# Block-pair loads of a matmul with rotary embedding: all in fp32 quarters over SyncE and ScalarE, in twelve groups instead of ten

## The chip, the core and the metric

The kernel runs on one core of one Trainium2 chip. The metric is the device time of one execution in microseconds (us), lower is better. The engines are named as in the profile: PE is TensorE (PEld its weight loads), DVE VectorE, ACT ScalarE, POOL GpSimd, SP SyncE. SP, ACT and POOL can issue DMA transfers; each has its own queue, and all queues are served by the same 16 DMA engines.

## What is computed

```python
x: (16, 512, 768) fp32, weight: (768, 768) fp32, cos, sin: (512, 64) fp32, n_heads = 12
y = np.matmul(x, weight).reshape(16, 512, 12, 64)
y1, y2 = y[..., :32], y[..., 32:]
out1 = y1 * cos1 - y2 * sin1      # cos1, sin1: first half of the head, cos2, sin2: second
out2 = y2 * cos2 + y1 * sin2
out = np.concatenate([out1, out2], axis=-1).reshape(16, 512, 768)
```

## The kernel before

The 8192 rows of x are cut into 64 tiles of 128 rows, in 16 groups of four (`QB`). The contraction of 768 is cut into six chunks of 128 (`CHUNKS`). The kernel computes in fp16 with fp32 sums, so each tile of x has to be loaded, cast to fp16 and turned (rows to columns) before PE can use it as the stationary operand. A group's result fills six PSUM banks (`py`).

There are two ways for the rows of x to get in.

- A plain tile: `load` (line 201) brings 128 x 768 fp32 by one DMA of SP, 384 KB in pieces of 3072 bytes; `cast` (236) makes fp16 on ACT; `turn_rows` (256) turns it on PE by twelve half-height transposes (line 266) and ACT copies the result out of PSUM (line 185 by way of `copy`).
- A block pair: the third and fourth tile of a group, which are two tiles of a batch pair, together. `load_quarter` (209) brings them in four DMAs, one for each 32 partitions, in pieces of 192 elements, so that a 32 x 32 block transpose on DVE (`turn_pair`, 282, line 294) is all the turning needed; PE and the PSUM copies are left out.

`BLOCKS` (137) says which pairs go that way: the second pair of groups 5 to 14, ten in all. In odd groups the quarters come over SP as fp32 in 768-byte pieces into one of three buffers `xb`, and ACT casts the pair in one instruction to `xd` (`cast_pair`, 274), which DVE then turns. In even groups POOL issues the quarters, the DMA casts on the way, fp16 pieces of 384 bytes land in one of three buffers `xh`, and DVE turns from there.

A matmul step takes one tile. In groups 1 to 14 each matmul uses 64 rows of the contraction, and two lines of them run through PE a little apart (`walk`, `one`, `both`; line 359). `rope` multiplies PSUM by cos and sin on DVE (line 411) and adds the halves on POOL (line 428) into `ov`, one of four group buffers. `store` (line 449) writes half a group, 768 KB, by one DMA, mostly issued by ACT.

Everything is ordered by hand. `Flow.do` gives an instruction to its engine in program order and adds the semaphore waits that its reads and writes need; so an instruction that waits holds back all that is behind it on its engine, and DMAs are issued by the engine's own instruction stream. The main loop runs over the tiles i = 4 to 63. In each step it gives PE the matmuls, then `bturns` (block pairs turned by DVE, four tiles ahead), `turns` (plain tiles, three to four ahead), `casts` (five ahead), `pool_loads` (the POOL quarters, 20 ahead), and the stores that the table `stores` (603) puts at this step. For groups 3 to 10 those are the steps 4(g+2) and 4(g+2)+2. SP's loads are a list of their own (`fetch`, 471): tiles in order, with one quarter put behind a tile from the group before a pair on; `pump` (487) issues from it whenever a cast has freed a buffer, with at most ten tiles and three pairs in hand.

In ACT's stream the order within four steps is: copy of the first plain tile turned, cast of the pair (in groups that have one over SP), copy of the second, a store, the casts of two plain tiles, a store.

The lines of the loop that set this order:

```python
        bturns(i + B_AHEAD)
        turns(i + 1 + (T_AHEAD if i > QB else 2), 1)
        casts(i + 1 + (C_AHEAD if i > QB else 4), 1 + i % 2)
        pool_loads(i + P_AHEAD)
        for q in stores.get(i, ()):
            store(*q)
```

Of the kernel before, what the change touches and what calls it, by code (L numbers as in the profile page):

```python
# [10 lines left out]
FP32 = mybir.dt.float32  # L11
FP16 = mybir.dt.float16
# [4 lines left out]
class Flow:  # L17
# [24 lines left out]
    def do(self, e, make, reads=(), writes=(), dma=None, tick=True, after=0):  # L42
        need = {}
        for k in reads:
            for s, v in self.wrote.get(k, {}).items():
                need[s] = max(need.get(s, 0), v)
        for k in writes:
            for d in (self.wrote, self.readby):
                for s, v in d.get(k, {}).items():
                    need[s] = max(need.get(s, 0), v)  # L50
        if e == "pe":
            need.pop("pe", None)
            if after:
                need["pe"] = after
        waits = self.settle(e, need)
        for s, v in waits[:-1]:
            self.eng[e].wait_ge(self.sem(s), v)  # L57
        i = make(self.eng[e])
        if waits:
            s, v = waits[-1]  # L60
            i.wait_op(self.sem(s), v, "sem-ge")
        name, step = (dma, 16) if dma else (e, 1)
        self.sem(name)
        at = self.count[name] + step
        if tick or dma:
            i.then_inc(self.sems[name], step)
            self.count[name] = at
            self.known[name, at] = dict(self.seen[e])
        for k in reads:
            d = self.readby.setdefault(k, {})  # L70
            d[name] = max(d.get(name, 0), at)
        for k in writes:
            self.wrote[k] = {name: at}
            self.readby[k] = {}
        return i
# [30 lines left out]
def kernel(  # L106
# [11 lines left out]
    f = Flow(nc, tc)  # L118
    do = f.do
    P = nc.NUM_PARTITIONS  # L120

    B, S, H = x.shape
# [4 lines left out]
    NQ = P // R  # L127
    NT = H // (2 * P)
    SB = S // P
    QB = 4  # L130
# [4 lines left out]


    BLOCKS = {}
    for g in range(5, 15):
        BLOCKS[g, 1] = "pool" if g % 2 == 0 and g >= 4 else "sp"

    def sbuf(name, shape, dt):
        return nc.alloc_sbuf_tensor(name, shape, dt).ap()

    NX, NB, NBH, NC, NCP, NXT, NXP, NOV = 10, 3, 3, 5, 2, 8, 4, 4

    ident = sbuf("ident", [P, P], FP16)
    cold = sbuf("cold", [P, 512], FP16)
# [3 lines left out]
    w_sb = sbuf("w_sb", [P, NT, 2, H], FP16)  # L151
    xs_b = [sbuf(f"xs{i}", [P, H], FP32) for i in range(NX)]
    xb_b = [sbuf(f"xb{i}", [P, 2 * H], FP32) for i in range(NB)]
    xh_b = [sbuf(f"xh{i}", [P, 2 * H], FP16) for i in range(NBH)]
    xc_b = [sbuf(f"xc{i}", [P, H], FP16) for i in range(NC)]
    xd_b = [sbuf(f"xd{i}", [P, 2 * H], FP16) for i in range(NCP)]
    xt_b = [sbuf(f"xt{i}", [P, NT, 2, P], FP16) for i in range(NXT)]
# [20 lines left out]
    def ring(name, n, state={}):  # L178
        k = state.get((id(f), name), 0)
        state[id(f), name] = k + 1  # L180
        return k % n
# [6 lines left out]
    def where(i):  # L188
        g, s = divmod(i, QB)
        return QB * (g // SB) + s, g % SB  # L190

    def pair_of(i):
        return i // QB, (i % QB) // 2

    def is_block(i):
        return pair_of(i) in BLOCKS

    xs, xc, xT = {}, {}, {}
# [10 lines left out]
    def load_quarter(gh, q):  # L209
        g, h = gh  # L210
        b, r = where(g * QB + 2 * h)
        e = BLOCKS[gh]
        src = x[b : b + 2].rearrange("b (j a r) (q k) -> r q a (b j) k", r=SB, a=R, q=NQ)
        if q == 0:
            xs[gh] = ring("xh", NBH) if e == "pool" else ring("xb", NB)
        k = xs[gh]
        name = f"xh{k}" if e == "pool" else f"xb{k}"
        buf = xh_b[k] if e == "pool" else xb_b[k]
        dst = buf.rearrange("p (j k) -> p j k", j=2 * NQ)
        do(e, lambda eng: eng.dma_start(out=dst[ts(q, R)], in_=src[r, q]),  # L220
           writes=[f"{name}q{q}"], dma=name)

    wv = weight.rearrange("(p t e) n -> t e p n", t=NT, e=2)

# [49 lines left out]
    def cast_pair(gh, e="act"):  # L274
        k = xs[gh]
        c = ring("xd", NCP)
        xc[gh] = c
        do(e, copy(e, xd_b[c].rearrange("p (t j e) -> p t j e", t=NT, e=2),
                   xb_b[k].rearrange("p (j t e) -> p t j e", t=NT, e=2)),
           reads=[f"xb{k}q{q}" for q in range(NQ)], writes=[f"xd{c}"])  # L280

    def turn_pair(gh):
        g, h = gh
        z = ring("xp", NXP)
        dst = xp_b[z].bitcast(FP32)
        if BLOCKS[gh] == "pool":
            k = xs[gh]
            src = xh_b[k].bitcast(FP32).rearrange("p (j t) -> p t j", t=NT)
            rd = [f"xh{k}q{q}" for q in range(NQ)]
        else:  # L290
            c = xc[gh]
            src, rd = xd_b[c].bitcast(FP32), [f"xd{c}"]
        v = xp_b[z].rearrange("p (t m e) -> p t e m", t=NT, e=2)
        do("dve", lambda eng: eng.transpose(out=dst, in_=src), reads=rd, writes=[f"xp{z}"])  # L294
        for s in (0, 1):
            xT[g * QB + 2 * h + s] = (
                lambda t, e, s=s: v[:, t, e, ts(s, P)], f"xp{z}")
# [171 lines left out]


    fetch, quarters = [], []
    soon = [p for p in sorted(BLOCKS) if BLOCKS[p] == "sp"]
    for i in range(QB, NTILE):
        if soon and i >= max(2, soon[0][0] - 1) * QB:
            quarters += [(soon[0], q) for q in (0, 2, 1, 3)]
            soon.pop(0)
        if not is_block(i):
            fetch.append(i)
            if quarters:
                fetch.append(quarters.pop(0))  # L480
        elif quarters and quarters[0][0] == pair_of(i):
            fetch.append(quarters.pop(0))
# [40 lines left out]
    def castx(i, e):  # L523
        cast(i, e)
        xs_used[0] += 1
# [33 lines left out]
    pump()  # L559

    rows_on = [False]
    state = {"cast": 4, "turn": 4, "bturn": 0, "pool": 0}
    pairs = sorted(BLOCKS)
    pool_pairs = [p for p in pairs if BLOCKS[p] == "pool"]

    def casts(upto, most=NTILE):
        while state["cast"] < min(upto, NTILE) and most > 0:
            most -= 1
            i = state["cast"]
            state["cast"] += 1  # L570
            if not is_block(i):
                castx(i, "act")
            elif i % 2 == 0 and BLOCKS[pair_of(i)] == "sp":
                cast_pair(pair_of(i))
                xb_used[0] += 1
            pump()
# [9 lines left out]
    def bturns(upto):  # L586
        while state["bturn"] < len(pairs):
            gh = pairs[state["bturn"]]
            if gh[0] * QB + 2 * gh[1] >= upto:
                return  # L590
            turn_pair(gh)
            state["bturn"] += 1

    def pool_loads(upto):
        while state["pool"] < len(pool_pairs):
            gh = pool_pairs[state["pool"]]
            if gh[0] * QB + 2 * gh[1] >= upto:
                return
            for q in (0, 2, 1, 3):
                load_quarter(gh, q)  # L600
            state["pool"] += 1

    stores = {}
    for g in range(LAST):
        for h in (0, 2):
            i = QB * (g + 1) + h
            q = (g, h * H, (h + 2) * H, "act")
# [4 lines left out]
            elif g < LAST - 2:  # L612
                i = QB * (LAST - 2) + 2 * (g - LAST + 4) + h // 2
            else:
                q = q[:3] + ("sp",)
            stores.setdefault(i, []).append(q)

    C_AHEAD, T_AHEAD, B_AHEAD, P_AHEAD = 5, 3, 4, 20

    for i in (0, 1):  # L620
        mm0(i, CHUNKS[5])
# [15 lines left out]
    for i in range(QB, NTILE):  # L637
        g, s = divmod(i, QB)
        us = units(g)
        done_to = (s + 1) * H  # L640
        rows_on[0] = QB <= i < QB * LAST - 1
        if g < LAST:
            if s % 2 == 0:
                for r in range(2):
                    lines[r].extend(walk(i // 2, r))
            for n in range(1, 4):
                both((i - QB) * 4608 + n * 1536)
                if n == 1 and i > QB:
                    turns(i + T_AHEAD, 1)
        if i == QB * LAST:  # L650
            both(NTILE * 4608)
        for p in pieces(g, s) if g == LAST else ():
            a, z, _, bank = p
            for c in CHUNKS:
                mm_piece(i, p, c, c == CHUNKS[0], c == CHUNKS[-1],
                         tick=c == CHUNKS[-1])
            for u in us:
                if u[1] == z:
                    rope(g, u)
        bturns(i + B_AHEAD)  # L660
        turns(i + 1 + (T_AHEAD if i > QB else 2), 1)
        casts(i + 1 + (C_AHEAD if i > QB else 4), 1 + i % 2)
        pool_loads(i + P_AHEAD)
        for q in stores.get(i, ()):
            store(*q)
        if g == LAST:
            if s == 2:
                store(g, 0, H, "sp")
            if s == 3:
                store(g, H, 2 * H, "act")  # L670
# [4 lines left out]
    for k, add in enumerate(late):  # L675
        c = 3 * H + 256 + 256 * k
# [38 lines left out]
```

## Time and profile before

| What | Value |
|---|---|
| Time, median of 3 runs | 152.34 us (152.06 to 155.32) |
| The profiled execution's own time | 151.85 us |
| Its span (first to last instruction) | 150.1 us |
| Granted TensorE clock, mean | 0.986 of full speed |
| Busy: PE, DVE, POOL, ACT | 140.7, 126.9, 123.0, 77.9 us |
| Bytes moved by DMA | 51.27 MB, 342 GB/s over the span |
| Queue of SP, of ACT, of POOL | 27.92, 21.10, 1.97 MB |
| Issue to landing, median: tile, fp32 quarter, fp16 quarter, store by ACT | 17.3, 17.4, 12.8, 8.8 us |
| Idle of ACT before its copies, waiting for PE's turns | 43.5 us |
| Idle of POOL before its adds, waiting for DVE | 18.8 us |

How to read it: a busy PE in the table does not say that PE is the bound; the chain of work that ended last does, since it follows each step back to what released it. The DMA view cut to a window counts, for each queue, the packets sent (the pieces of the transfers, and small closing ones), the bytes, and the share of the time of 16 DMA engines; the shares of several queues overlap and can sum to more than 100%. The bytes of POOL's queue are those written (fp16); it reads twice as many. In the timeline an engine's rows show start, length, line, what is written from what, and in brackets the idle time ahead with what ended it; rows with a q behind the engine (ACTq, SPq) are DMA issues.

### The profile page before, as it was taken

How to read it: one execution, taken by the hardware profiler on the slowest of the kernel's cores; microseconds unless marked ns; L12 is line 12 of the kernel's file. 1: busy time of each engine (PE TensorE's matmuls, PEld its weight loads, DVE VectorE, ACT ScalarE, POOL GpSimd, SP SyncE). 2: the span in 40 equal slices, each digit the busy share in tenths (PEclk: the TensorE clock that was granted, in tenths of full speed). 3: DMA queues.
4: the chain of work that ended last, by engine and by line, in shares of the span. 5: the costliest groups of instructions: out<-in, count | busy, mean ns of one | idle time of the engine just before them, and what ended most of it. 6: DMA issues, size and time to landing. Idle time of an engine off the chain costs nothing.

```text
span 150.1 us, 4381 instructions
## 1 busy us (share of the span) xinstructions
PE 140.7 (94%) x1938; PEld 101.4 (68%) x1938; DVE 126.9 (85%) x92; ACT 77.9 (52%) x92; POOL 123.0 (82%) x68
## 2 busy tenths in 40 slices
PE   6879999999999999999999999999999999999930
PEld 2445567777787777777777777777777777776620
DVE  0245989887888899999999998999989998999990
ACT  3453888787777924456262905293327626264000
POOL 1000495999989988999999999999996979999990
PEclk9999999999999999999999999999999999999995
DMA  4999999999999999999999999999999999966574
GB/s 125 393 391 398 404 401 390 274 404 275 319 367 327 347 354 361 285 397 332 359 346 392 355 332 359 370 391 319 356 367 412 415 406 399 385 269 235 217 296 144
DMA packets 27556, 51.27 MB, mean 342 GB/s; under 512 B 7185, under 2 KB 13073, under 8 KB 27537
## 3 DMA queue, kind: packets, MB, share of 16 engines
q1 hardware_dynamic: 14592, 27.92, 53.8%
q10 hardware_dynamic: 7504, 21.10, 35.5%
q0 software_dynamic: 5440, 1.97, 10.6%
q8 instruction: 15, 0.25, 0.6%
q14 instruction: 5, 0.03, 0.1%
HBM read 27.79 MB, written 25.17 MB: 353 GB/s over the span
## 4 chain that ended last, share of the span: by engine, by line
PE 87%; DMA 4%; DVE 4%; SPq 1%; issue 1%; ACT 1%; DVEq 0%
PE py L359 73%; PE py L334 8%; PE pt L266 4%; DMA w_raw<-in_weight_dram 4%; DVE tq L411 2%; PE pt L251 1%; DVE ov L428 1%; SPq L205 1%; SPq L227 1%; ACT xt L185 1%; DVE xs L411 0%; DVE w_sb L185 0%; SPq L710 0%; DVEq L57 0%; SPq L116 0%
## 5 line engine op out<-in xcount | busy, mean ns | idle before, releaser
L428 POOL TENSOR_TENSOR ov<-tq 128x1536 f32<-128x1536 f32 (+3 forms) x30 | 76.3, 2564 | 18.9 <-DVE tq L411 18.8
L359 PE MATMUL py<-w_sb,xt 64*128 64x256 f16 (+1 forms) x864 | 80.7, 323 | 0.0
L411 DVE TENSOR_TENSOR tq<-py,csn 128x1024 f32<-128x1024 f32 (+2 forms) x46 | 74.8, 1656 | 5.4 <-PE py L359 5.0
L359 PEld LDWEIGHTS py<-w_sb,xt 64*128 64x128 f16 x864 | 53.2, 94 | 17.8 <-DVE tq L411 0.4
L185 ACT COPY xt<-pt 128x768 f16<-128x768 f16 x42 | 33.6, 801 | 47.8 <-PE pt L266 43.5
L359 PE MATMUL py<-w_sb,xp 64*128 64x256 f16 (+1 forms) x480 | 46.8, 323 | 0.0
L185 ACT CAST xc<-xs 128x768 f16<-128x768 f32 x44 | 39.1, 909 | 12.1 <-DMA xs<-in_x_dram 12.0
L411 DVE TENSOR_TENSOR w_raw<-py,csn 128x1024 f32<-128x1024 f32 (+1 forms) x21 | 35.2, 1676 | 4.4 <-PE py L359 4.2
L428 POOL TENSOR_TENSOR ov<-w_raw 128x1536 f32<-128x1536 f32 (+1 forms) x12 | 35.0, 2926 | 3.6 <-DVE w_raw L411 3.4
L359 PEld LDWEIGHTS py<-w_sb,xp 64*128 64x128 f16 x480 | 30.4, 94 | 9.5
L334 PE MATMUL py<-w_sb,xt 128*128 128x256 f16 (+1 forms) x90 | 15.7, 323 | 1.3 <-DVE w_sb L185 1.1
L266 PEld LDWEIGHTS pt<-ident,xc 64*128 64x128 f16 x432 | 14.1, 95 | 1.9 <-ACT xt L185 0.6
L334 PEld LDWEIGHTS py<-w_sb,xt 128*128 128x128 f16 x90 | 8.1, 98 | 7.2 <-DVE w_sb L185 2.7
L266 PE MATMUL pt<-ident,xc 64*128 64x64 f16 x432 | 12.3, 190 | 0.3 <-ACT xt L185 0.3
L220 POOL DMA_DIRECT2D xh<-in_x_dram x20 | 11.7, 590 | 0.0
L185 ACT CAST xd<-xb 128x1536 f16<-128x1536 f32 x5 | 8.2, 1637 | 0.0
L294 DVE STREAM_TRANSPOSE xp<-xh 128x768 f32<-128x768 f32 x5 | 6.2, 1241 | 0.0
L510 PE MATMUL py<-cold 128*128 128x512 f16 x12 | 4.8, 569 | 1.4 <-DVE cold L453 1.4
L185 DVE CAST w_sb<-w_raw 128x768 f16<-128x768 f32 x6 | 3.3, 558 | 3.3 <-DMA w_raw<-in_weight_dram 3.3
L185 DVE COPY xt<-pt 128x768 f16<-128x768 f16 x2 | 1.1, 558 | 5.2 <-PE pt L251 5.2
L294 DVE STREAM_TRANSPOSE xp<-xd 128x768 f32<-128x768 f32 x5 | 4.8, 969 | 0.0
L251 PEld LDWEIGHTS pt<-ident,xc 128*128 128x128 f16 x48 | 3.2, 104 | 2.1 <-ACT xc L185 1.3
(16 smaller groups left out, 14.5 us busy)
## 6 DMA issues: line engine op xcount, KB each, us to landing
out_dram<-ov ACTq DMA_DIRECT2D x26, 768.0 KB, 8.8
xs<-in_x_dram SPq DMA_DIRECT2D x44, 384.0 KB, 17.3
xb<-in_x_dram SPq DMA_DIRECT2D x20, 192.0 KB, 17.4
out_dram<-ov SPq DMA_DIRECT2D x4, 768.0 KB, 3.7
w_raw<-in_weight_dram SPq DMA_DIRECT2D x6, 384.0 KB, 6.9
xh<-in_x_dram POOLq DMA_DIRECT2D x20, 96.0 KB, 12.8
out_dram<-ov SPq DMA_DIRECT2D x1, 384.0 KB, 2.3
out_dram<-ov ACTq DMA_DIRECT2D x1, 384.0 KB, 2.3
```

The lines of the kernel that those rows point to most:

```text
L185: eng.copy(out=o, in_=i_) if e == "act" else eng.tensor_copy(out=o, in_=i_)
L205: do(e, lambda eng: eng.dma_start(out=xs_b[k], in_=x[b].rearrange("(p r) h -> r p h", r=SB)[r]), writes=[f"xs{k}"], dma=f"xs{k}")
L220: do(e, lambda eng: eng.dma_start(out=dst[ts(q, R)], in_=src[r, q]), writes=[f"{name}q{q}"], dma=name)
L227: do(e, lambda eng: eng.dma_start(out=w_raw[:, t, h], in_=wv[t, h]), writes=[f"wr{t}{h}"], dma=f"w{t}{h}")
L251: do("pe", lambda eng: eng.transpose(pt[:, t, h, :], src[:, t, h, :], ident), reads=[f"xc{c}", "ident"], writes=[f"pt{k}"], tick=(t, h) == ...
L266: do("pe", lambda eng: eng.transpose(pts[r][:, t, h, :], src[rows, t, h, :], ident[rows, rows]), reads=[f"xc{c}", "ident"], writes=[f"pt{r ...
L294: do("dve", lambda eng: eng.transpose(out=dst, in_=src), reads=rd, writes=[f"xp{z}"])
L334: do("pe", lambda eng: eng.matmul(ps, get(t, h), w_sb[:, t, h, a - s * H : z - s * H], start=start, stop=stop), reads=[key, f"w{t}{h}"], w ...
L359: do("pe", lambda eng: eng.matmul(py[:, a:z], get(t, h)[rows], w_sb[rows, t, h, a - s * H : z - s * H], start=start, stop=not opens and en ...
L411: do("dve", lambda eng: eng.tensor_tensor(out=tq.rearrange("p j (h d) -> p j h d", d=D), in0=ps.rearrange("p (h d) -> p h d", d=D) .unsque ...
L428: do(adder, lambda eng: eng.tensor_tensor(out=ov_b[o][:, ds(c0, w)].rearrange("p (h t d) -> p h t d", t=2, d=HD), in0=tq[:, 0].rearrange(" ...
L510: do("pe", lambda eng: eng.matmul(py[:, ts(b, 512)], cold[:, 0:P], cold, start=True, stop=warmed[0] < WARM - 6), reads=["cold"], writes=[f ...
```

## The change

- `BLOCKS` now holds the second pair of groups 3 to 14, twelve pairs, all fp32; POOL issues no loads, and the fp16 buffers `xh` are gone. There are four `xb` buffers for three.
- Of each pair, quarters 0 and 1 are issued by SP out of the `fetch` list, and quarters 2 and 3 by ACT, in the main loop after the casts of a step and ahead of its stores. Quarter 2 is issued 11 tile steps and quarter 3 nine tile steps before the pair's first tile (later for the first pairs: from steps 4 and 5 on). The cast of a pair waits for all four quarters, as before.
- All pairs are cast by ACT into `xd` and turned by DVE from there.

```diff
-    for g in range(5, 15):
-        BLOCKS[g, 1] = "pool" if g % 2 == 0 and g >= 4 else "sp"
+    for g in range(3, 15):
+        BLOCKS[g, 1] = "sp"
...
-    NX, NB, NBH, NC, NCP, NXT, NXP, NOV = 10, 3, 3, 5, 2, 8, 4, 4
+    NX, NB, NC, NCP, NXT, NXP, NOV = 10, 4, 5, 2, 8, 4, 4
...
     def load_quarter(gh, q):
         g, h = gh
         b, r = where(g * QB + 2 * h)
-        e = BLOCKS[gh]
         src = x[b : b + 2].rearrange("b (j a r) (q k) -> r q a (b j) k", r=SB, a=R, q=NQ)
-        if q == 0:
-            xs[gh] = ring("xh", NBH) if e == "pool" else ring("xb", NB)
-        k = xs[gh]
-        name = f"xh{k}" if e == "pool" else f"xb{k}"
-        buf = xh_b[k] if e == "pool" else xb_b[k]
-        dst = buf.rearrange("p (j k) -> p j k", j=2 * NQ)
+        k = xs[gh] = sorted(BLOCKS).index(gh) % NB
+        dst = xb_b[k].rearrange("p (j k) -> p j k", j=2 * NQ)
+        e = "sp" if q < 2 else "act"
         do(e, lambda eng: eng.dma_start(out=dst[ts(q, R)], in_=src[r, q]),
-           writes=[f"{name}q{q}"], dma=name)
+           writes=[f"xb{k}q{q}"], dma=f"xb{k}{e}")
...
-            quarters += [(soon[0], q) for q in (0, 2, 1, 3)]
+            quarters += [(soon[0], q) for q in (0, 1)]
...
-            elif i % 2 == 0 and BLOCKS[pair_of(i)] == "sp":
+            elif i % 2 == 0:
                 cast_pair(pair_of(i))
...
+    pieces_at = {}
+    for n, (g, h) in enumerate(pairs):
+        for q, lead in ((2, 11), (3, 9)):
+            pieces_at.setdefault(max(QB + 2 * n + q - 2, g * QB + 2 * h - lead), []).append(((g, h), q))
...
-        pool_loads(i + P_AHEAD)
+        for piece in pieces_at.get(i, ()):
+            load_quarter(*piece)
         for q in stores.get(i, ()):
             store(*q)
```

## The prediction

> **What bounds the kernel now.** I read the chain of work that ended last first, then the timeline of ScalarE (ACT) and VectorE (DVE), then the DMA view cut to short windows. In the chain in order of time (start, length, what):
>
> ```profile
> 40.42 1.95 PE py L359 x18
> 42.37 0.18 PE pt L266 x10
> 42.55 1.95 PE py L359 x19
> ...
> 59.20 5.85 PE py L359 x56
> 65.05 0.17 PE pt L266 x12
> 65.22 1.95 PE py L359 x18
> 67.17 0.18 PE pt L266 x10
> 67.34 5.85 PE py L359 x56
> ```
>
> From 18 to 134 us the chain is TensorE (PE) without a hole. A group without a block pair repeats every 8.50 us (34.05 to 42.55), one with a pair every 8.14 (59.20 to 67.34): two 0.17 to 0.18 us turns are missing. So the kernel is bound by PE, and a transfer matters only once it comes too late. How late may it come? ACT and DVE around the cast of pair (13,1):
>
> ```profile
> 112.40 0.90 ACT L185 CAST xc<-xs 128x768 f16<-128x768 f32 x1 [2.64 <-DMA xs<-in_x_dram]
> 114.19 0.80 ACT L185 COPY xt<-pt 128x768 f16<-128x768 f16 x1 [0.89 <-PE pt L266]
> 114.89 1.65 ACT L185 CAST xd<-xb 128x1536 f16<-128x1536 f32 x1
> 116.32 0.38 ACTq L449 DMA_DIRECT2D out_dram<-ov  x1
> ```
> ```profile
> 117.45 1.23 DVE L411 TENSOR_TENSOR tq<-py,csn 128x1024 f32<-128x1024 f32 x1 [0.27 <-PE py L359]
> 118.59 0.97 DVE L294 STREAM_TRANSPOSE xp<-xd 128x768 f32<-128x768 f32 x1
> ```
>
> The cast ends at 116.54 and DVE wants its result at 118.59: 2.05 us to spare, and DVE itself idles about 0.4 us in such a group (0.27 here, 0.41 before its next product). A later cast holds DVE, DVE holds the PSUM banks, and PE has no hole to take that in. ACT already waits 2.64 us for a plain load: the DMA side has little left. The DMA view of four windows (60 to 62, 80 to 84, 26 to 27.8, 114 to 122):
>
> ```profile
> DMA packets 647, 0.58 MB, mean 290 GB/s; under 512 B 349, under 2 KB 550, under 8 KB 646
> q1 hardware_dynamic: 312, 0.42, 70.0%
> q0 software_dynamic: 312, 0.11, 46.1%
> ```
> ```profile
> DMA packets 770, 1.61 MB, mean 402 GB/s; under 512 B 74, under 2 KB 308, under 8 KB 770
> q10 hardware_dynamic: 370, 1.08, 67.3%
> q1 hardware_dynamic: 371, 0.51, 34.7%
> ```
> ```profile
> DMA packets 266, 0.38 MB, mean 210 GB/s; under 512 B 22, under 2 KB 183, under 8 KB 266
> ```
> ```profile
> DMA packets 1179, 3.31 MB, mean 414 GB/s; under 512 B 105, under 2 KB 105, under 8 KB 1178
> ```
>
> q1 is SP's queue, q10 ACT's, q0 GpSimd's (POOL). Two things are to be seen. Queues that both have work send equally many packets (312 and 312, 371 and 370), whatever their size. And the 768-byte pieces of the quarters are slow when nothing large runs beside them (210 and 290 GB/s), but free when the other queue sends 3072-byte packets (402 against 414).
>
> **The change, part by part.**
>
> *Two more pairs, groups 3 and 4.* Each takes two PE turns off the chain: 8.50 less 8.15 is 0.35 us, twice 0.70. DVE gets 2 transposes of 0.97; at 31.00 to 39.50 its four products fill 7.04 of 8.50 us, so 0.97 fits, as it does in the groups that have a pair now. This is the whole gain on the chain.
>
> *ACT's computing.* Seven more CAST xd at 1.637 are 11.5 us, four CAST xc at 0.909 and four COPY at 0.801 fall away (6.8): 4.7 more on an engine that is 52% busy and waits 43.5 us for PE's turns. Cost 0 by itself; the cover is that waiting.
>
> *POOL.* 20 issues at 0.590 (11.7 us, between the adds) go. POOL's adds are followed by stores, not by PE; PE, DVE and ACT never wait for POOL. Gain 0; next behind the adds are the products they wait for (18.8 us in the waits). Five DVE transposes drop from 1.241 to 0.969: 1.4 us less in all, on an engine that the chain does not pass there. Gain 0.
>
> *SP.* 40 tile loads for 44 and 24 quarters for 20, at about 0.43 us each: no change of issue time. Three quarters now stand ahead of tile 13. At 26 to 27.8 SP alone sends 266/16 = 16.6 packets per DMA engine in 1.8 us, 0.108 each; a quarter is 256/16 plus one closing packet, 17, so 1.84 us, three 5.5. Tile 13 was issued at 11.7 and took 13.2: from 24.9 it goes to about 30.4, against its cast at 30.56. Later tiles are as tight, but a cast comes two tiles, some 4 us, before its PE turn: 0.
>
> *Quarters 2 and 3 on ACT.* The 24 issues of about 0.43 us lie beneath running casts and copies, as the stores' do (a store is issued at 108.17 beneath the copy of 108.17). They wait for the cast four pairs back, long done. But in ACT's queue they stand in line with the stores. In the code the order of each group of four steps is: cast of pair n, quarter 3 of pair n+1, store, quarter 2 of pair n+2, store. Quarter 3 is thus issued right behind one pair's cast, and the next cast, one group (8.15 us) later, waits for it. If it takes longer, that cast is late, the next quarter 3 is issued late too, and the loop runs at the pace of ACT's queue. Queued behind a waiting cast are ACT's copy of the second turned tile, two casts and two stores; PE wants that copy and those casts 4 to 5 us later (next turn at 122.1), so DVE's 2.05 us end first.
>
> Latency with nothing ahead: the nearest rows are POOL's first quarters of a batch, 7.6 to 10.0 us to landing. I take 7.6, as four of the five lie by 8, leaving 8.15 - 7.6 = 0.55. Allowance before PE loses time: 0.55 + 2.05 + 0.4 = 3.0 us.
>
> Pace of ACT's queue, two stores and two quarters a group, 17 packets per engine each. From 80 to 84: 370/16 = 23.1 packets in 4 us, 0.173 each beside SP, so 2.94 a store. A small packet beside SP's mix, from 60 to 62: 312/16 = 19.5 in 2 us, 0.103; from 36 to 38, where the view counts 267 and 265, 0.120; mean 0.111, a quarter 1.89. Sum 2 x 2.94 + 2 x 1.89 = 9.66 us a group, if SP always has something queued; its loads take 17.4 us to land, so at first it has. SP needs only 52 packets a group (two tiles of 9, two quarters of 17) and gets 68 in that time. If only 52 of ACT's 68 share, that is 52/68 x 9.66 = 7.39, and the other 16 alone take about 0.113 each (0.108 small, 0.119 large at 414 GB/s), 1.8: 9.2 us. The lowest end is bytes alone: 3.15 MB a group at 402 GB/s is 7.8, below 8.15, no loss. I take the middle of 9.2 and 9.66, 9.43: 1.28 us too slow per group. Stores come twice a group from step 20 on, and seven casts, pairs 8 to 14, follow: 7 x 1.28 = 9.0, less 3.0, is 6.0 us of PE time. POOL's queue hid its small packets in a third turn; here they take turns from the stores.
>
> The Trainium skill ("DMA: Bandwidth & Descriptors", section "Specifications") gives 512 B as the smallest transfer at line rate. By it a 768 B piece would cost its bytes only, and the sum would be the lowest end. The trace disagrees: 210 GB/s.
>
> *Sum.* The profiled execution took 151.85 us (span 150.1), 0.5 below the median of 152.34. 151.85 - 0.70 + 6.0 = **157.1 us**.
>
> **Rivals.**
>
> 1. *The queue keeps up: not slower.* Small pieces meet the other queue's large ones, as at 80 to 84, and 7.8 us a group suffices; quarter 3 lands in 7.6. For it: 402 GB/s there, and the SP queue no longer shares with POOL. Against it: both queues have their small pieces in every group. It decides below 8.15 us a group. 151.85 - 0.70 = 151.15. The Trainium skill (same page, "Issuing engines are not separate DMA queues") also says that issuing from several engines only saves issue time. By that rule too the move from POOL to ACT would leave this time; the trace shows equal turns per queue, so it does matter who queues where.
> 2. *Slower queue, mostly absorbed.* At 8.7 us a group, 7 x 0.55 = 3.9, less 3.0: 0.9, so 152.0.
> 3. *SP never runs dry and the queue falls behind from pair 6 on:* 9 x 1.51 = 13.6, less 3.0: 10.6, so 161.7. For it: 17.4 us of SP backlog; against it: few stores before step 20.
> 4. *The relief elsewhere shows:* over 2% faster would need 3 us off a chain that is PE's own work; only 0.70 are in sight.
>
> **How the numbers follow.** Forecast (153 to 161.5) 0.54, rival 1 0.29, rival 2 0.11, rival 3 and beyond 0.04, rival 4 0.02. The likeliest is 157.1. For 8 in 10 the range takes in rival 1 and nearly all of rival 3: 150.8 to 161.7. About 2% is what a measurement of this kernel can tell; from 152.34 that is 149.3 and 155.4. Of the forecast 0.08 lies below 155.4. Slower: 0.46 + 0.04 = 0.50; same: 0.29 + 0.11 + 0.08 = 0.48; faster 0.02.
>
> **What would show it.** Right: ACT's cast xd waiting for xb, more from pair to pair; landing of the xb issues on ACT above 8.15 us; DVE's transpose waiting for ACT, holes in PE from about 75 us on; period above 8.15. The 0.70 shows as 8.15 us groups 3 and 4. Wrong: cast xd never waiting, ACT's quarters landing within 8 us and a GB/s row near 400 throughout; that is rival 1. Holes in PE before 40 us would mean that the early SP loads, which I priced at nothing, came too late.

## The result, and the profile after

The changed kernel takes 158.86 us (median of 4 runs, 158.56 to 162.10), the kernel before 153.11 (median of 4, 152.06 to 155.32): 1.0395 times as long, 95% interval 1.0342 to 1.0449. Runs more than 1.5% above the fastest of the same kernel are left out of this ratio and of those below, so it isn't the quotient of the medians. The profiled execution took 158.95 us, span 157.1, 7.0 more than before's 150.1, at a granted clock of 0.992 (before 0.986): the clock isn't the cause.

From the page of the changed kernel: span, busy engines, GB/s in 40 slices, the two queues, the chain's shares, ACT's casts of the pairs (busy, mean, idle before), and the issues with their median time to landing.

```profile
span 157.1 us, 4304 instructions
...
PE 141.6 (90%) x1890; PEld 113.1 (72%) x1890; DVE 127.4 (81%) x94; ACT 82.1 (52%) x91; POOL 111.6 (71%) x48
...
GB/s 146 321 396 401 362 210 329 240 348 362 369 373 383 322 342 362 391 387 388 394 400 401 394 394 398 397 396 377 390 362 399 309 304 291 357 241 240 228 304 153
...
q1 hardware_dynamic: 15104, 27.14, 50.6%
q10 hardware_dynamic: 14032, 25.82, 44.5%
...
PE 50%; DMA 29%; DVE 6%; POOL 4%; issue 3%; ACTq 2%; SPq 1%; ACT 1%; DVEq 0%; POOLq 0%
...
L184 ACT CAST xd<-xb 128x1536 f16<-128x1536 f32 x12 | 19.5, 1623 | 13.2 <-DMA xb<-in_x_dram 13.2
...
xb<-in_x_dram SPq DMA_DIRECT2D x24, 192.0 KB, 11.4
xb<-in_x_dram ACTq DMA_DIRECT2D x24, 192.0 KB, 9.9
```

PE's busy time grew by 0.9 us, the span by 7.0. In before the chain was PE from 18 to 134 us; here 29% of it is DMA (25% loads into xb, the rest the weights, as in before), and the chain in order of time (start, length, what) shows which:

```profile
33.95 10.67 DMA xb<-in_x_dram
44.64 9.69 DMA xb<-in_x_dram
54.36 0.33 ACT xd L184
...
61.28 9.87 DMA xb<-in_x_dram
71.18 8.87 DMA xb<-in_x_dram
80.07 0.33 ACT xd L184
```

Each of these transfers is a quarter 3, issued by ACT at the moment the cast before it starts (44.64 starts as the one of 33.95 ends): the loop of the prediction, at 8.87 to 10.67 us a turn where a group of PE work takes 8.15. Who waits, over the whole execution (total, times, longest):

```profile
ACT xd L184 <- DMA xb<-in_x_dram: 13.2, 7, 3.5
...
PE py L349 <- ACT xt L184: 4.6, 5, 2.2
...
DVE xp L284 <- ACT xd L184: 2.0, 2, 1.5
```

And the largest hole, in the timeline of the changed kernel from 112 to 120 us (in brackets the idle time ahead and what ended it):

```profile
115.18 1.58 ACT L184 CAST xd<-xb 128x1536 f16<-128x1536 f32 x1 [3.55 <-DMA xb<-in_x_dram]
115.19 0.32 ACTq L215 DMA_DIRECT2D xb<-in_x_dram  x1
...
116.65 0.81 ACT L184 COPY xt<-pt 128x768 f16<-128x768 f16 x1
116.79 0.98 DVE L284 STREAM_TRANSPOSE xp<-xd 128x768 f32<-128x768 f32 x1 [1.48 <-ACT xd L184]
...
117.60 2.75 PE L349 MATMUL py<-w_sb,xt 64*128 64x512 f16 x29 [2.19 <-ACT xt L184]
```

The cast stands 3.55 us for its last quarter; behind it on ACT stands the copy of 116.65, which PE needs for its next tile; PE stands 2.19 us. DVE waits too (1.48), but PE is stopped by the copy, not by DVE.

Where the 7 us lie is seen by setting the start of each projection matmul after against that of the same matmul before (worked out from the two traces, us; the last column is near the end; the two lines of matmuls that run side by side differ by up to 0.2):

```
before, us       23     27     35     43     47     55     77     82    108    112    143
later by, us  +0.53  +1.56  +1.93  +1.58  +1.79  +3.34  +3.95  +4.71  +4.71  +7.16  +7.27
```

The first 0.53 is the start (in the twelve other runs it lies between -0.54 and +0.79 at 23 us). The steps before 27 and before 35 are two holes of their own, ahead of the first late cast (below); the fall to 43 is the first pair's gain. Between 43 and 47 the second pair's gain and the first late cast meet, and the steps after that are late casts. So 7.27 = 0.53 (start) + 1.03 and 0.37 (the two holes) - 0.70 (two pairs) + 6.0 (the rest, late casts).

### The profile page after: what moved, and what is told of

Its sections match the earlier page's. It is cut to its first block, busy times and chain, and to the rows that moved or that the text cites. A ratio compares the mean times of both kernels' runs of the same rounds, so it can differ in the third digit from the quotient of the medians.

```text
span 157.1 us, 4304 instructions
## 1 busy us (share of the span) xinstructions
PE 141.6 (90%) x1890; PEld 113.1 (72%) x1890; DVE 127.4 (81%) x94; ACT 82.1 (52%) x91; POOL 111.6 (71%) x48
## 4 chain that ended last, share of the span: by engine, by line
PE 50%; DMA 29%; DVE 6%; POOL 4%; issue 3%; ACTq 2%; SPq 1%; ACT 1%; DVEq 0%; POOLq 0%
PE py L349 38%; DMA xb<-in_x_dram 25%; PE py L324 8%; DMA w_raw<-in_weight_dram 4%; POOL ov L418 4%; DVE tq L401 4%; PE pt L261 3%; ACTq L439 2%; PE pt L246 1%; DVE ov L418 1%; SPq L204 1%; ACTq L215 1%; DVE xp L284 1%; SPq L222 1%; ACT xt L184 1%
## 5 line engine op out<-in xcount | busy, mean ns | idle before, releaser
L349 PE MATMUL py<-w_sb,xt 64*128 64x256 f16 (+1 forms) x768 | 75.9, 323 | 5.3 <-ACT xt L184 4.6
L349 PE MATMUL py<-w_sb,xp 64*128 64x512 f16 (+1 forms) x576 | 57.3, 323 | 0.0
L184 ACT COPY xt<-pt 128x768 f16<-128x768 f16 x38 | 30.4, 802 | 40.4 <-PE pt L261 36.2
L349 PEld LDWEIGHTS py<-w_sb,xp 64*128 64x128 f16 x576 | 43.2, 94 | 4.9
L184 ACT CAST xc<-xs 128x768 f16<-128x768 f32 x40 | 34.9, 910 | 9.4 <-DMA xs<-in_x_dram 9.3
L184 ACT CAST xd<-xb 128x1536 f16<-128x1536 f32 x12 | 19.5, 1623 | 13.2 <-DMA xb<-in_x_dram 13.2
L261 PE MATMUL pt<-ident,xc 64*128 64x64 f16 x384 | 14.2, 190 | 0.5 <-ACT xt L184 0.3
L284 DVE STREAM_TRANSPOSE xp<-xd 128x768 f32<-128x768 f32 x12 | 11.6, 970 | 2.0 <-ACT xd L184 2.0
L246 PE MATMUL pt<-ident,xc 128*128 128x128 f16 x48 | 4.0, 220 | 0.9 <-ACT xc L184 0.9
L500 PEld LDWEIGHTS py<-cold 128*128 128x128 f16 x12 | 1.4, 130 | 3.4 <-issue 1.9
```

The lines of the kernel that those rows point to most:

```text
L184: eng.copy(out=o, in_=i_) if e == "act" else eng.tensor_copy(out=o, in_=i_)
L246: do("pe", lambda eng: eng.transpose(pt[:, t, h, :], src[:, t, h, :], ident), reads=[f"xc{c}", "ident"], writes=[f"pt{k}"], tick=(t, h) == ...
L261: do("pe", lambda eng: eng.transpose(pts[r][:, t, h, :], src[rows, t, h, :], ident[rows, rows]), reads=[f"xc{c}", "ident"], writes=[f"pt{r ...
L349: do("pe", lambda eng: eng.matmul(py[:, a:z], get(t, h)[rows], w_sb[rows, t, h, a - s * H : z - s * H], start=start, stop=not opens and en ...
L500: do("pe", lambda eng: eng.matmul(py[:, ts(b, 512)], cold[:, 0:P], cold, start=True, stop=warmed[0] < WARM - 6), reads=["cold"], writes=[f ...
```

## The experiments

Three questions: which part of the change costs the time; what makes the quarters slow; and whether a lead or a queue repairs it. "Wait" is ACT's wait of cast xd for xb.

**1. Ten pairs in place of twelve, on the new queues.**

```diff
-    for g in range(3, 15):
+    for g in range(5, 15):
```

> The changed kernel with ten pairs (groups 5 to 14) in place of twelve. Queue theory (as predicted: ACT's queue needs 9.4 us a group from step 20 on, and each third quarter waits one group): the loop is untouched, only the 0.7 us of the two pairs is lost, 158 to 160 us, and cast xd waits as often. Early theory (at 16 to 32 us the changed kernel's DMA runs at some 283 GB/s against 400 and 335 before, because the first quarters meet no large packets; it is 1.6 MB behind at 32 us and never gets that back): the loss goes with the two pairs, 152 to 154 us, cast xd waits less than 4 us in all. Lead theory (8.15 us of lead are less than the 8 to 11 us a quarter takes on ACT's queue, whatever its load): 157 to 159.

Measured: 154.49 us, ratio 1.0104 (1.0067 to 1.0141). PE runs level with before up to 108 us, and then there is one hole:

```profile
109.38 1.58 ACT L184 CAST xd<-xb 128x1536 f16<-128x1536 f32 x1 [3.06 <-DMA xb<-in_x_dram]
```
```profile
111.80 3.51 PE L349 MATMUL py<-w_sb,xt 64*128 64x512 f16 x40 [1.65 <-ACT xt L184]
```

So the two early pairs bring with them three quarters of the loss, though by themselves they take 0.70 us off PE. The seven casts at a steady 1.28 us too slow, which the prediction had, are not there: with ten pairs on the same queues three casts are late, and PE stands for one of them.

**2. The longer lead.**

```diff
-        for q, lead in ((2, 11), (3, 9)):
+        for q, lead in ((2, 15), (3, 13)):
```

> The changed kernel with quarters 2 and 3 issued by ACT 15 and 13 tile steps ahead in place of 11 and 9. Queue theory: one more group of lead is 8.15 us of allowance against some 9 us of lateness, 152 to 153.5. Early theory: the bytes are as late as before, the missing 1.6 MB now show in the tile loads or the casts all the same, 155 to 158. Lead theory: no cast waits for a quarter, 152 to 152.5 (the hole at 27 us stays).

Measured: 155.67 us, 1.0226 (1.0176 to 1.0277). No cast xd waits any more, and the 0.70 is there: PE is 0.71 us ahead of before from 47 to 85 us. Then it loses 4.2 us between 85 and 108. The waits of this kernel say where:

```profile
ACT xc L184 <- issue: 9.2, 8, 2.2
ACT xc L184 <- DMA xs<-in_x_dram: 7.1, 4, 2.2
```

ACT stands in its DMA issues (9.2 us, not in the changed kernel) and then waits for plain tiles. The lead breaks the loop. That the early lack of bytes (317 GB/s from 18 to 34 us, where before has 368) is what comes out here, later and at another place, fits run 3 but isn't shown by itself.

**3. Ten pairs with the longer lead** (both edits).

> The ten-pair kernel with quarters 2 and 3 issued 15 and 13 steps ahead: both cures at once. Early theory: no loss early, and the late quarter near 112 us has 8 us more: 151.5 to 152.3, the same as before. Queue theory: 9 us of lateness against 11 of allowance: 151.9 to 152.5. If a longer lead only moves the wait to the tile loads, 153 to 154.5.

Measured: 152.33 us, 1.0012 (0.9990 to 1.0035), no late cast, PE at a constant +0.52 from 17 us to the end. The move of the quarters from SP and POOL to SP and ACT costs nothing when the lead is long and the early pairs are absent.

**4. The two early pairs alone, on the queues of before** (`range(3, 15)` in the kernel before: group 3 by SP, group 4 by POOL).

> The kernel before with twelve pairs (group 3 over SP, group 4 over POOL) and nothing else changed. Queue theory: no quarter stands behind a store, the two pairs give their 0.70: 151.2 us beside 151.9 of before. Early theory: four quarters of pair 3 on SP alone and four of pair 4 on POOL at 16 to 35 us cost the DMA about as much as in the changed kernel, 153 to 156. Lead theory: 151.2.

Measured: 156.07 us, 1.0205 (1.0133 to 1.0277). The early pairs cost 2% without any quarter on ACT's queue; here plain tiles are late:

```profile
ACT xc L185 <- DMA xs<-in_x_dram: 34.1, 16, 4.5
```

**5. Quarters 2 and 3 by POOL** (the edit of 2, and):

```diff
-        e = "sp" if q < 2 else "act"
+        e = "sp" if q < 2 else "pool"
```

> The changed kernel with quarters 2 and 3 issued by POOL, in fp32, 15 and 13 tile steps ahead; differs from the run with the lead of 15 and 13 (155.3 to 156.2) in the issuing queue alone. Queue theory: with a third queue no quarter stands behind a store and each queue has its turn: 151.5 to 153. Early theory: the first quarters run as small packets beside small packets all the same: 154 to 156.5.

Measured: 156.67 us, 1.0317 (1.0284 to 1.0350), with plain tiles late by 40.3 us in 17 waits. A third queue doesn't help; what is slow is not the place in ACT's line.

**6. Large pieces in quarters 2 and 3.**

```diff
-        do(e, lambda eng: eng.dma_start(out=dst[ts(q, R)], in_=src[r, q]),
+        if q < 2:
+            into, frm = dst[ts(q, R)], src[r, q]
+        else:
+            into = xb_b[k][ts(q, R)].rearrange("p (b h) -> p b h", b=2)
+            frm = x[b : b + 2, r * P + q * R : r * P + (q + 1) * R].rearrange("b p h -> p b h")
+        do(e, lambda eng: eng.dma_start(out=into, in_=frm),
```

> Quarters 2 and 3 fetched as pieces of 3072 bytes: same bytes, same queue, same instants, a quarter of the packets; the rows land in another order, so half of each pair holds other data. Queue theory: two stores and two quarters of five packets take 2 x 2.94 + 2 x 0.87 = 7.6 us a group, below 8.15, no cast waits: 152 to 153. Early theory: only ACT's share of the early small packets goes, SP's stays: 154 to 156. Lead theory: a quarter is 1 us shorter, about 8 us, so a part of the waits stays: 153 to 156.

Half of each pair then holds other rows, so this kernel leaves out the function's result and serves for the time alone. Measured: 156.1 us, 1.0217 (1.0148 to 1.0285). About half of the change's loss is left, with half of the quarters still in small pieces; that left the piece size open, and run 7 was made for it.

**7. Large pieces in all quarters of the two early pairs** (as 6, for groups 3 and 4).

> The changed kernel (twelve pairs) with all four quarters of the first two pairs (groups 3 and 4) fetched as pieces of 3072 bytes: same bytes, queues and instants, other rows in those two pairs. Early theory, by packet size: the DMA keeps near 400 GB/s at 16 to 32 us, what is left is the hole near 112 us less the 0.7 of the two pairs: 152.5 to 154. Rival (it is the bytes of the quarters ahead of the tiles, or ACT's queue from pair 5 on, and not the size of the pieces): 156.5 to 159.

These two pairs hold other rows, and again only the time counts. Measured: 159.46 us, 1.0409 (1.0359 to 1.0459), as slow as the change. The DMA view of 18 to 34 us:

```profile
DMA packets 2033, 4.98 MB, mean 311 GB/s; under 512 B 240, under 2 KB 480, under 8 KB 2031
```

Only 480 packets under 2 KB (the change has 1970 there), and still far below 400 GB/s. The small pieces, to which the prediction had put the slowness, are not the main cause of it. Why large pieces in the later pairs took back half of the loss in run 6 stays open: sent in a fourth of the packets, they may wait less in ACT's queue.

**8. Small pieces over all partitions.** The number, the size, the queues and the instants of all transfers are those of the change; each quarter's 256 pieces go to 128 partitions, two to each, in place of 32 partitions with eight. They come from neighbouring rows, so the pairs hold other data and the function's result is left out.

```diff
-        do(e, lambda eng: eng.dma_start(out=dst[ts(q, R)], in_=src[r, q]),
+        into = xb_b[k][:, q * 384 : (q + 1) * 384].rearrange("p (b c) -> p b c", b=2)
+        frm = x[b : b + 2, r * P : (r + 1) * P, q * 192 : (q + 1) * 192].rearrange("b p c -> p b c")
+        do(e, lambda eng: eng.dma_start(out=into, in_=frm),
```

> The changed kernel (twelve pairs) with each quarter written over all 128 partitions instead of 32: same bytes, same 768-byte pieces and their number, same queues and instants; other data lie in the pairs. Partition theory (a transfer into 32 partitions runs at some 210 to 300 GB/s when nothing else is in flight, whatever its pieces; large pieces into 32 partitions did not help): the DMA stays near 400 GB/s at 16 to 32 us and later, few or no late casts: 151.2 to 153.5. Piece theory, as in the prediction (768-byte pieces are slow): 157 to 159 as the changed kernel. Queue-order theory (a quarter stands behind the stores, whatever the rate): 155 to 159.

Measured: 151.67 us, 0.9961 (0.9944 to 0.9978). No cast xd waits; these casts come every 8.15 us to the end:

```profile
33.34 1.62 ACT L184 CAST xd<-xb 128x1536 f16<-128x1536 f32 x1
41.49 1.64 ACT L184 CAST xd<-xb 128x1536 f16<-128x1536 f32 x1
49.64 1.63 ACT L184 CAST xd<-xb 128x1536 f16<-128x1536 f32 x1
...
122.99 1.65 ACT L184 CAST xd<-xb 128x1536 f16<-128x1536 f32 x1
```

PE is 0.65 us behind at 35 us (the start) and 0.05 ahead from 47 on: that is the 0.70. The DMA view from 18 to 34 us, of before, of the change and of this kernel:

```profile
DMA packets 2594, 5.89 MB, mean 368 GB/s; under 512 B 225, under 2 KB 841, under 8 KB 2592
```
```profile
DMA packets 2953, 4.39 MB, mean 275 GB/s; under 512 B 218, under 2 KB 1970, under 8 KB 2951
...
q1 hardware_dynamic: 2303, 3.65, 89.6%
```
```profile
DMA packets 4031, 6.09 MB, mean 380 GB/s; under 512 B 294, under 2 KB 2647, under 8 KB 4029
...
q1 hardware_dynamic: 3021, 4.73, 81.6%
```

SP's packets are about as long on the average in both (3.65 MB / 2303 = 1585 bytes, 4.73 / 3021 = 1566), but one takes 0.896 x 16 x 16 us / 2303 = 0.100 us in the change and 0.069 here. The engines are busy in both; in the change each packet takes 1.4 times as long. That holds for SP's 768-byte packets (54.5 against 37.3 ns, worked out from the traces) and as much for its 3072-byte packets (182 against 129), which belong to tile loads into 128 partitions: the quarters slow down what is in flight beside them. In these 16 us the change moves 1.5 MB less than before. From 63 to 106 us its GB/s row reads 387 to 401, and PE's pace asks for 3.15 MB / 8.15 us = 386: next to nothing is left over to make 1.5 MB good (some 4 us of DMA time).

The Trainium skill ("SBUF — State Buffer", section "Door 1: The DMA port swizzle (why `[64,N]` ≈ `[32,N]`)") says that a transfer goes as fast as the SBUF ports that its partitions reach: partitions 0 to 31, and also 0 to 63, reach half of the 16 ports, some 218 GB/s at most. The traces agree in the direction, but the 210 GB/s of before is not a quarter by itself: from 26 to 27.8 us SP's queue alone had work, 161 pieces of 768 bytes and 83 of 3072. The prediction had set this row against the 512-byte rule of the skill's "DMA: Bandwidth & Descriptors" ("Specifications"); that objection falls, since 768-byte pieces are part of 380 GB/s here.

**9. The queues take the halves crosswise** (SP quarters 0 and 2, ACT 1 and 3).

```diff
-        e = "sp" if q < 2 else "act"
+        e = "sp" if q % 2 == 0 else "act"
...
-            quarters += [(soon[0], q) for q in (0, 1)]
+            quarters += [(soon[0], q) for q in (0, 2)]
...
-        for q, lead in ((2, 11), (3, 9)):
-            pieces_at.setdefault(max(QB + 2 * n + q - 2, g * QB + 2 * h - lead), []).append(((g, h), q))
+        for q, lead in ((1, 11), (3, 9)):
+            pieces_at.setdefault(max(QB + 2 * n + q // 2, g * QB + 2 * h - lead), []).append(((g, h), q))
```

> The changed kernel with quarters 0 and 2 issued by SP and 1 and 3 by ACT, so that each queue alternates between the lower and the upper 64 partitions instead of staying in one half. If SP's two quarters in the same half are what slows the DMA at 16 to 32 us: 154 to 157. If any 32 partitions are slow alone, no difference: 157.5 to 160.

Measured: 163.32 us, 1.0768 (1.0669 to 1.0867), the other way than expected:

```profile
ACT xd L184 <- DMA xb<-in_x_dram: 21.0, 10, 4.1
```

In the change SP writes only partitions 0 to 63 and ACT only 64 to 127 with their quarters, so that two quarters under way from the two queues never write the same half; here they often do. That fits the destination as the cause, and would mean that two transfers to different halves disturb each other less than two to the same half. It isn't a proof by itself, since the quarters' order changed too.

**10. The last tile loads held back, first try** (ten pairs, and):

```diff
-                if xs_sent[0] - xs_used[0] >= NX:
+                if xs_sent[0] - xs_used[0] >= (NX if j < 56 else 6):
```

> The ten-pair kernel with SP's last six tile loads (tiles 56 to 63) held back to six tiles in hand in place of ten, so that they don't leave in one burst. With ten pairs all of the loss is one hole of 1.9 us at 112 us, when a quarter on ACT's queue is late. Burst theory: at 100 to 108 us SP sends only 3072-byte packets and each packet of ACT has to wait for one, so ACT's queue gets 290 and 318 packets in 4 us where it got 585 before; without the burst the hole goes: 0.5 to 0 us below the kernel before, 151.3 to 152.3. Queue theory as predicted (lateness that grows by some 1.3 us a group whatever SP sends): the hole stays, 153 to 154.5.

Measured: 155.8 us, 1.0227 (1.0172 to 1.0282). The edit did not do what it was for: six loads still left SP in one burst at 95.24 us. So in effect this is run 1 again, with the hole at 112, and it is 1.2% slower than run 1, outside both intervals. A difference of that size between two late-cast kernels may be scatter.

**11. The last six loads tied to casts** (ten pairs; each load of tile 56 and later also waits for the newest cast, so they leave between 95 and 114 us):

```diff
+    gate = [None]
...
-            writes=[f"xs{k}"], dma=f"xs{k}")
+            reads=[gate[0]] if i >= 56 else [], writes=[f"xs{k}"], dma=f"xs{k}")
...
+        gate[0] = f"xc{c}"
```

> The ten-pair kernel with SP's last six tile loads each made to wait for a cast some 16 us later (in the first try the loads kept their order on SP and left in the same burst, so nothing was held back). Burst theory: without six tile loads in flight at 100 to 108 us ACT's queue keeps its 290 packets per 2 us, the quarter of pair 13 lands in time, no hole at 112 us: 151.6 to 152.8. Queue theory as predicted (lateness that grows group by group): the hole of 1.9 to 2.2 us stays, 153.5 to 155.5.

Measured: 154.06 us, 1.0120 (1.0041 to 1.0200). The wait of run 1 at 109 us shrinks from 3.06 to 1.24 and PE's hole from 1.9 to 0.2 us, but PE loses 0.87 us between 41 and 82 us, where run 1 lost nothing. Without the burst of SP's last loads that hole all but goes; the total doesn't, it is run 1's within the intervals.

**12. The change's own rows and pieces over all partitions.** Each quarter becomes two loads of 96 KB, each for 128 partitions.

```diff
-        do(e, lambda eng: eng.dma_start(out=dst[ts(q, R)], in_=src[r, q]),
-           writes=[f"xb{k}q{q}"], dma=f"xb{k}{e}")
+        for j in (2 * q, 2 * q + 1):
+            do(e, lambda eng, j=j: eng.dma_start(out=dst[:, j], in_=src[r, :, :, j]),
+               writes=[f"xb{k}j{j}"], dma=f"xb{k}{e}")
...
-           reads=[f"xb{k}q{q}" for q in range(NQ)], writes=[f"xd{c}"])
+           reads=[f"xb{k}j{j}" for j in range(2 * NQ)], writes=[f"xd{c}"])
```

> The changed kernel with the same rows, the same 768-byte pieces and the same queues and steps, but cut the other way: each of the four loads of a pair becomes two of 96 KB, and each of these fills all 128 partitions instead of 32 (the source of one is 4 by 32 pieces, for the four 192-element parts of 32 rows). Nothing is left out. Theory (the 32-partition destination is what slows the loads): as in e9_spread_partitions, casts xd never wait, 18 to 34 us runs at 370 to 390 GB/s, the groups repeat every 8.15 us and the 0.70 us shows: 151.0 to 152.3 us, ratio 0.990 to 1.000. Rival 1 (it was the source side: e9_spread_partitions also read 128 neighbouring rows in place of 32, and here the reads are the change's own again): 275 to 310 GB/s at 18 to 34 us, late casts, 156 to 160 us. Rival 2 (the doubled number of issues, 24 more of about 0.43 us on ACT and as many on SP, is not hidden: ACT stands blocked in its issues as in e2_lead_15_13, or copies slip behind them): no late casts xd, but 153 to 155.5 us.

Measured: 222.19 us, 1.4599 (1.4533 to 1.4664): all three expectations fall. The DMA view of this kernel from 48.5 to 51 us, while PE stands still:

```profile
DMA  2222222222222222222222222222222222222222
...
DMA packets 309, 0.23 MB, mean 92 GB/s; under 512 B 8, under 2 KB 309, under 8 KB 309
...
q10 hardware_dynamic: 155, 0.12, 13.7%
q1 hardware_dynamic: 154, 0.12, 13.6%
```

Both queues have work, and together they keep 27% of 16 DMA engines busy, some four. The source of these loads is four columns of 32 pieces. The Trainium skill ("DMA: Bandwidth & Descriptors", section "Why a DMA increments its semaphore by 16 and not by 1") says that a DMA is spread over the largest number of engines, up to 16, that divides the slowest dimension of both its access patterns, and that they are the lowest-numbered; by that it is four here, the same four for both queues, and the trace agrees with four (92 GB/s, 27%); which four, it doesn't show. So this run doesn't test the theory: it takes the destination's limit away and brings a worse one.

## Why the prediction was right, and where it wasn't

- *The chain and its bound*: right. Where casts are on time, groups repeat every 8.15 us (run 8).
- *Two more pairs, -0.70*: right as PE's own work (runs 2 and 8 show 0.70 to 0.71 in two steps). In the change the first, 0.35, lies between 35 and 39 us, and the second comes in two halves of 0.18, at 44 and 46 us, around the first late cast.
- *ACT computing, POOL, ACT's issues at 0*: nothing in the change speaks against it (with the longer lead of run 2 ACT's issues did cost, 9.2 us). Run 3 has them all on the new queues, for ten pairs, at the time of before.
- *Quarter 3 issued right behind the last cast, a self-timed loop*: right as the way in which late bytes reach PE in the change, but not the whole reason for the sign: run 1 keeps the loop and is 1.0% slower, run 2 has no late cast and is 2.3% slower. The casts xd came every 8.79 us on the average (34.23 to 122.14, ten intervals), predicted 9.43, wanted 8.15.
- *DVE's 2.05 us end first*: wrong. PE waits for ACT's second copy, which the prediction gave 4 to 5 us of slack; it is behind the cast in ACT's line and PE waited for it in all five late-cast holes. In run 8, where no cast is late, this copy ends at 109.03 us and PE's first matmul that needs it starts at 110.27: 1.2 us of slack, less than DVE's 2.05. The prediction had looked at PE's next turn, not at that matmul.
- *9.0 of slowness less 3.0 of allowance, +6.0*: the size held (6.0 by the lag table), the working didn't, so that the two agree is luck. The slowness is not a steady 1.28 us from step 20 on: the first late cast is at 44.64, and the holes are at 47, 57, 74, 83 and 118 us. The pace per packet came from rows with 32-partition loads under way, so it had their slowness in it, put to another cause.
- *768-byte pieces are slow*: this is the step that failed. Run 7 has large pieces and is slow; run 8 has small pieces over 128 partitions and isn't. What the slow runs share is the destination of 32 partitions; before and run 3 have it too, for ten pairs, and lose nothing, so it costs time only where the early pairs or the short lead leave no slack. The row that the prediction rested on did not say what it was read to say: of its 266 packets 83 were large, and they carried two thirds of the 0.38 MB.
- *SP's early quarters at 0*: wrong, as the prediction's own sign for it (holes before 40 us) came: holes at 27 and 36 us, though not late tiles ended them (below), and 275 GB/s in place of 368 from 18 to 34. The early pairs cost 3.3 us with the long lead (run 2 against 3: 155.67 less 152.33), 4.4 with the short one (158.86 less 154.49).
- *POOL's third queue hid its small packets*: not borne out; in run 5 POOL issues quarters again and nothing is gained.

The point lay 1.85 us below the profiled execution (158.95): the start (0.53) and the two early holes (1.03 and 0.37), none of which it had, make up that difference (1.93 in all).

Open: what ended the two early holes. The profile calls both "issue" (0.66 us ahead of the matmul of 27.60, 0.20 ahead of the turn of 35.72). They go with the time at which packets of the instruction queue (q8) left. Of before, the change and all runs but 12, those whose first packet left by 23.4 us lose nothing at 27 us; the five with a later one lose 0.2 us (run 5, 23.8), 0.45 (run 7, 23.9), 0.85 (run 4, 23.9), 1.03 (the change, 25.0) and 1.1 (run 6, 25.3). At 35 us only the change and run 6 lose time, and only there the second packet left after 33 us. Late instructions, held up on the slowed DMA engines, are thus likely, not shown. Open too is the source side: of two batches, run 8 reads 128 neighbouring rows where the change reads every fourth of 512, and run 12, which was to part the two, didn't. That run 7, with 32 neighbouring rows in 32 partitions, is as slow as the change speaks against the source.

No version beats the kernel before beyond the 0.4% of run 8, which loads other rows and leaves out the function's result; run 3 is level with it. A way to fill 128 partitions with the change's own data and keep all 16 DMA engines was not tried.

## What to carry to other kernels

Here transfers that land in 32 partitions held the DMA engines 1.4 times as long for each packet, those of other loads too, so before small pieces are blamed for a slow load, look at how many partitions it fills, and at how many engines its outermost dimension divides into. A load issued behind the consumer of the load before it, with a lead of one period, makes a loop that runs at the load's latency. Where the DMA side runs within 3% of what the kernel asks (386 of some 395 GB/s), as here, there is next to nothing to make up bytes lost early: they come out later as waits, which a longer lead only moves.

## What the runs showed of the hardware

- SP's packets took 1.4 times as long (0.100 against 0.069 us, about the same mean size) when the quarters landed in 32 partitions in place of 128 (the spacing of the rows read changed too), with the DMA engines shown as busy in both: a busy share of 90% did not tell the rate.
- Two queues whose 32-partition transfers often write the same half of the partitions cost 163.3 us, against 158.9 with the halves kept apart (the quarters' order differs too). The skill's "SBUF — State Buffer" (section "Can I just issue two DMAs to hit both halves?") gives two transfers, one to each half, only 6% over one; no run here measures the pair alone.
- A load with an outermost dimension of four ran on about four DMA engines, 92 GB/s with two queues at work.
- ACT, with four more steps of lead on its loads, stood 9.2 us in its own DMA issues, which took no such time before.
